# The last layer's first feed-forward product in seven block products instead of eight

## The chip, the cores and the metric

The kernel runs on one core of one Trainium2 chip. The metric is the device time of one execution in microseconds (us). The engines go by these names in the rows: PE is TensorE (matmuls), PEld its weight loads, DVE is VectorE, ACT is ScalarE, POOL is GpSimd, SP is SyncE, which issues the DMA transfers.

## The reference

The program is one inference step through a trunk of two layers over 640 tokens (512 latent tokens and 128 context tokens), 1024 channels wide. Each layer has four token mixers and then a gated feed-forward part. The change touches only the feed-forward part of the second, last layer:

```python
h2 = rms_norm(x) * (1 + sc2) + sh2
a, gate_ffn = jnp.split(h2 @ p['w_ffn_in'], 2, axis=-1)
x = x + g2 * ((jax.nn.silu(gate_ffn) * a) @ p['w_ffn_out'])
```

`w_ffn_in` has 1024 rows (k) and 2 x 2816 columns, a linear and a gate half; `w_ffn_out` has 2816 rows and 1024 columns. After the last layer `y = rms_norm(x, final_gain)`. Everything is float32.

## The kernel before

**Numbers in two parts.** Every fp32 operand of a large product is split in a high part (rounded to the type that the rows call fp32r, on ACT, L84) and a low part (the difference, on VectorE, L176, for weights L123). A product is three matmuls per 128 rows of k: high by high, high by low, low by high. Tokens lie along the columns, channels along the 128 partitions.

**Feed-forward part.** The function `layer` works it off as follows. `out` is the output projection with its residual; `norm_mod` (L1047 to L1061) computes the modulated norm of one half of the tokens into the tiles `hh` and `hl` and runs woven with `out` and with the first two hidden blocks. The halves are 384 and 256 columns (`HALVES`). `hidden(j)` makes one of 22 blocks of 128 hidden columns: it loads the gate block `wg` and the linear block `wa` (`wload`: a 512 KB DMA into a raw buffer `wraw`, of which there are two; the high part `whi` by ACT and the low part `wlo` by VectorE, three buffers each). Then for each half: 24 matmuls with the gate (k has 8 tiles), tanh on ACT (L1210), one VectorE step (L1211), 24 matmuls with the linear block, one VectorE step (L1213), and the split of the result into `fh` and `fl`. So a block has 96 matmuls, 48 of 384 columns and 48 of 256.

**Groups.** Hidden blocks come in groups of 8, 8 and 6 (`KGROUPS`). After each of the first two groups `back` multiplies the group by `w_f2` (eight row blocks, each loaded by `wload`, 128 x 1024) and adds the result to the residual `x` (`resid`, L1070). The last group's `w_f2` blocks are kept in `wkh` and `wkl`, and its products run woven with the final norm.

**What sets the order.** A scheduler places each engine's instructions by its own estimates, near the order in which the program is written; `weave` mixes two streams in the program itself. Each engine then runs its list strictly in order and waits on semaphores. Buffers of a pool come free when their last reader is done; a DMA into a buffer waits on SP for that.

**PSUM.** Matmul results go to three tiles of 512 columns named `psg`, three named `pst` and one of 1024 named `pss`.

The functions that the diff touches:

Of the kernel before, what the change touches and what calls it, by code (L numbers as in the profile page):

```python
# [64 lines left out]
class Trunk:  # L65
# [1113 lines left out]
    def layer(self, l, hs, first):  # L1179
# [20 lines left out]
        def hidden(j, halves, tiles):  # L1200
            if tiles is None:
                tiles = fs[j] = self.u("fh", F32R), self.u("fl", F32R)
            hi, lo = tiles
            wg = self.wload(A["w_f1"][l, j, 1], 8, 128)
            wa = self.wload(A["w_f1"][l, j, 0], 8, 128)
            for c0, c1 in halves:
                y, tg = self.u("fy"), self.u("ft")
                n = c1 - c0
                pg = self.gemm(wg, hs, c0, c1)
                nc.scalar.activation(tg[:, 0:n], pg, AF.Tanh, scale=0.5)  # L1210
                nc.vector.scalar_tensor_tensor(tg[:, 0:n], tg[:, 0:n], 1.0, pg, op0=ALU.add, op1=ALU.mult)  # L1211
                pa = self.gemm(wa, hs, c0, c1)
                nc.vector.scalar_tensor_tensor(y[:, 0:n], tg[:, 0:n], 0.5, pa, op0=ALU.mult, op1=ALU.mult)  # L1213
                self.split(hi[:, c0:c1], lo[:, c0:c1], y[:, 0:n])
                self.drop(y, tg)
                yield 48 * n

        def some(half):
            for j in range(2):
                yield from hidden(j, (half,), fs.get(j))  # L1220

        fs = {}
        n0, n1 = (c1 - c0 for c0, c1 in HALVES)
        sum(out(*HALVES[0]))
        self.weave(self.norm_mod(hs, x, l, 24, 32, *HALVES[0]), out(*HALVES[1]), 8 * 24 * n1, 6)
        self.drop(ms)
        self.weave(self.norm_mod(hs, x, l, 24, 32, *HALVES[1]), some(HALVES[0]), 96 * n0, 6)
        sum(some(HALVES[1]))
        nxt = l + 1 < self.depth
        def ada():  # L1230
            if l == 0:
                yield from self.ada_tail(0, 40, 48, 2, 4, True)
            if nxt:
# [2 lines left out]
        ada = ada()

        def back(halves, last=False):
            for m in range(8):
                if last:  # L1240
                    if len(ws) <= m:
                        self.wload(A["w_f2"][l, m, :, g0:g1], g1 - g0, 128, kept=ws)
                    w = [z.rearrange("p (a b) -> p a b", b=128) for z in ws[m]]
                else:
                    w = self.wload(A["w_f2"][l, m, :, g0:g1], g1 - g0, 128)
                for c0, c1 in halves:
                    self.resid(x[m], self.gemm(w, [fs[j] for j in range(g0, g1)], c0, c1), l, 40, m, c0, c1)
                    yield 3 * (g1 - g0) * (c1 - c0)
# [287 lines left out]
```

## Time and profile before

| | us |
|---|---|
| Median of three runs (lowest, highest) | 3148.22 (3145.90, 3150.94) |
| The profiled execution | 3147.23 |
| Its span, first to last instruction | 3145.3 |
| TensorE busy in the span | 3038.9 (97%) |
| VectorE busy | 2174.5 (69%) |
| ACT busy | 1464.8 (47%) |
| GpSimd busy | 285.7 (9%) |

The mean granted clock of TensorE is 0.996 of full speed. The shares are means over stages that differ, attention and scan on the one side and large products on the other. Durations in the rows come from the one profiled execution.

### The profile page before, as it was taken

To read this page: it belongs to the slowest core of one execution; us is meant where nothing else is said; L and a number is where in the kernel's file an instruction comes from. 1 tells how busy PE (TensorE), PEld (TensorE's weight loads), DVE (VectorE), ACT (ScalarE), POOL (GpSimd) and SP (SyncE) were. 2 spreads that over 40 slices of the span, in tenths; PEclk is the share of its full clock that TensorE was granted. 3 is DMA by queue.
4 is the path that set the end of the run, shared out by engine and by line. 5 is a ranking of instruction groups with operands and counts; after the bars stand their busy time and mean duration, and the time that the engine had idled before them with its cause. 6 is when DMAs were issued, how large, how long until landed. Compare 5 with 4: busy or idle time off the path is not lost.

```text
span 3145.3 us, 54163 instructions
## 1 busy us (share of the span) xinstructions
PE 3038.9 (97%) x20898; PEld 2928.7 (93%) x20898; DVE 2174.5 (69%) x4894; ACT 1464.8 (47%) x3088; POOL 285.7 (9%) x301
## 2 busy tenths in 40 slices
...
GB/s 217 91 88 112 99 101 65 79 96 86 46 39 61 134 154 165 150 154 154 159 85 61 59 71 74 70 56 100 98 62 38 51 69 158 97 81 74 75 78 70
DMA packets 135121, 297.16 MB, mean 94 GB/s; under 512 B 15888, under 2 KB 53584, under 8 KB 134864
## 3 DMA queue, kind: packets, MB, share of 16 engines
...
## 4 chain that ended last, share of the span: by engine, by line
PE 71%; DVE 15%; ACT 5%; issue 4%; DMA 3%; POOL 1%; SPq 0%; DVEq 0%; ACTq 0%; POOLq 0%
PE psg L78 58%; PE pss L78 7%; PE pst L81 2%; PE pst L78 2%; DVE wlo L123 2%; ACT P L235 2%; DVE pl L176 1%; DMA ada<-in_w_ada 1%; DVE trash L984 1%; DVE sm L218 1%; DVE P L232 1%; DMA wraw<-in_w_f 1%; ACT whi L84 1%; PE pst L167 1%; DVE nx L1054 1%
## 5 line engine op out<-in xcount | busy, mean ns | idle before, releaser
L78 PE MATMUL psg<-hh,whi 128*128 128x384 f32 (+1 forms) x3776 | 1119.4, 315 | 9.8 <-DVE ft L1211 4.7
L78 PE MATMUL psg<-hl,whi 128*128 128x384 f32 (+1 forms) x3776 | 1108.2, 312 | 2.9 <-DVE hl L1056 2.3
L78 PEld LDWEIGHTS psg<-hh,whi 128*128 128x128 f32 x3776 | 715.8, 190 | 13.2 <-DVE ft L1211 5.3
L78 PEld LDWEIGHTS psg<-hl,whi 128*128 128x128 f32 x3776 | 716.3, 190 | 5.3 <-DVE hl L1056 3.0
L78 PE MATMUL psg<-hh,wlo 128*128 128x384 f32 (+1 forms) x3744 | 648.9, 312 | 0.0
L84 ACT ACTIVATE whi<-wraw 128x1024 fp32r<-128x1024 f32 (+3 forms) x402 | 380.9, 948 | 462.0 <-PE psg L78 366.7
L78 PEld LDWEIGHTS psg<-hh,wlo 128*128 128x128 f32 x3744 | 569.6, 190 | 0.1
L123 DVE TENSOR_TENSOR wlo<-wraw,whi 128x1024 fp32r<-128x1024 f32 (+3 forms) x398 | 453.5, 1140 | 125.3 <-ACT whi L84 111.1
L235 ACT ACTIVATE P<-pss,sm 128x768 f32<-128x768 f32 (+2 forms) x240 | 162.9, 680 | 208.7 <-DVE sm L218 120.9
L176 DVE TENSOR_TENSOR pl<-pst,ph 128x384 fp32r<-128x384 f32 (+2 forms) x408 | 196.8, 510 | 21.4 <-ACT ph L84 17.5
L84 ACT ACTIVATE ph<-pst 128x384 fp32r<-128x384 f32 (+2 forms) x408 | 170.7, 457 | 52.5 <-PE pst L81 49.1
L81 PE MATMUL pst<-ident,P 128*128 128x128 f32 x1104 | 168.8, 276 | 20.5 <-DVE of L242 15.4
L1070 DVE SCALAR_TENSOR_TENSOR xr<-psg,mod,xr 128x128 f32<-128x128 f32 (+1 forms) x192 | 78.5, 435 | 151.1 <-PE psg L78 151.1
L81 PEld LDWEIGHTS pst<-ident,P 128*128 128x128 f32 x1104 | 125.5, 141 | 36.2 <-DVE of L242 21.2
L984 DVE CUSTOM_DVE_ANT_0 yada<-ada 128x512 f32<-128x512 f32 x224 | 154.4, 689 | 5.1
L78 PE MATMUL psg<-oTh,whi 128*128 128x384 f32 (+1 forms) x512 | 152.1, 315 | 0.1
L218 DVE TENSOR_REDUCE sm<-pss 128x1 f32<-128x768 f32 x128 | 121.9, 952 | 42.9 <-PE pss L78 41.8
L78 PE MATMUL psg<-oTl,whi 128*128 128x384 f32 (+1 forms) x512 | 151.5, 312 | 0.0
L78 PE MATMUL psg<-fh,whi 128*128 128x256 f32 (+1 forms) x512 | 148.2, 309 | 0.0
L78 PE MATMUL psg<-fl,whi 128*128 128x256 f32 (+1 forms) x512 | 148.2, 309 | 0.0
L84 ACT ACTIVATE fh<-fy 128x384 fp32r<-128x384 f32 (+1 forms) x88 | 41.5, 471 | 179.1 <-DVE fy L1213 179.1
L1213 DVE SCALAR_TENSOR_TENSOR fy<-ft,psg 128x384 f32<-128x384 f32 (+1 forms) x88 | 42.9, 487 | 111.9 <-PE psg L78 111.3
...
## 6 DMA issues: line engine op xcount, KB each, us to landing
wraw<-in_w_f SPq DMA_DIRECT2D x128, 512.0 KB, 3.4
...
ada<-in_w_ada SPq DMA_DIRECT2D x112, 256.0 KB, 3.0
wraw<-in_w_br SPq DMA_DIRECT2D x64, 256.0 KB, 2.6
...
```

The lines of the kernel that those rows point to most:

```text
L78: self.nc.tensor.matmul(out, lhsT, rhs, start=start, stop=stop)
L81: self.nc.tensor.transpose(out, in_, self.ident)
L84: self.nc.scalar.activation(out, in_, AF.Copy, scale=scale)
L123: nc.vector.tensor_sub(lo[:, :n], raw[:, :n], self.r(hi[:, :n]))
L167: self.nc.tensor.transpose(ps[:, i * rows : (i + 1) * rows], t[:rows, c0 + i * 128 : c0 + (i + 1) * 128], self.ident[:rows, :rows])
L176: self.nc.vector.tensor_sub(lo, src, self.r(hi))
L218: nc.vector.tensor_reduce(nm, S[:, 0:n], axis=AX.X, op=ALU.max, negate=True)
L232: nc.vector.tensor_scalar_mul(P[:, p0 : p0 + n], P[:, p0 : p0 + n], l)
L235: self.nc.scalar.activation(P, S, AF.Exp, bias=nm, accum_out=l)
L984: nc.vector.tensor_tensor_reduce(out=y, in0=w, in1=c, scale=1.0, scalar=0.0, op0=ALU.mult, op1=ALU.add, accum_out=acc[:, b, k, j : j + 1])
L1070: self.nc.vector.scalar_tensor_tensor(x[:, a:b], ps[:, a - c0 : b - c0], mod[:, b_g + m, j : j + 1], x[:, a:b], op0=ALU.mult, op1=ALU.add)
L1213: nc.vector.scalar_tensor_tensor(y[:, 0:n], tg[:, 0:n], 0.5, pa, op0=ALU.mult, op1=ALU.mult)
```

## The change

In the last layer the tokens are cut into two equal halves of 320 (`EVEN`). Blocks 0 and 1 are computed as before, but in these halves. For each block j from 2 to 21 the weight is seen as two by two blocks: gate and linear by the lower and upper half of k (four k tiles each). a11 is the gate with k tiles 0 to 3, a12 the gate with 4 to 7, a21 and a22 the same of the linear weight. The tokens give b11, b12 (lower k, first and second half of tokens) and b21, b22 (upper k). Seven products of 12 matmuls of 320 columns replace eight: 84 matmuls a block. For that, GpSimd makes four combinations of the weights (s1 = a21 + a22, s2 = s1 - a11, s3 = a11 - a21, s4 = a12 - s2) per block, and these and the plain blocks are split; four combinations of the tokens (t1 = b12 - b11, t2 = b22 - t1, t3 = b22 - b12, t4 = b21 - t2) are made and split once (`sums`), woven with the second half of blocks 0 and 1. The results are put together by copies from PSUM on ACT (c11, c12, c22) and adds on VectorE. `norm_even` keeps the norm in fp32 beside its split. The groups are four, of 5, 6, 6 and 5 blocks (`SGROUPS`), so there are three `back` passes before the kept one, not two. The first layer's code is only moved into functions (`back`, `glu`, `hidden`, `ffn`). Lines up to the feed-forward part stand two or three further down (L78 is now L80, L84 L86, L123 L125, L176 L178, L1070 L1073).

The core of the diff:

```diff
+EVEN = ((0, 320), (320, 640))
...
+SGROUPS = ((0, 5), (5, 11), (11, 17), (17, 22))
...
-        nt = n // 128
+        at = [min(i, n - 128) for i in range(0, n, 128)]
+        nt = len(at)
...
-        for g0, g1 in KGROUPS:
-            for j in range(max(g0, 2), g1):
-                sum(hidden(j, HALVES, None))
-                for _ in range(4):
-                    next(ada, None)
-            if g1 < NH:
-                sum(back(HALVES))
-                self.drop([fs[j] for j in range(g0, g1)])
...
+            ada, groups = ada(), KGROUPS
+            last = self.ffn(l, x, ms, out, fs, ada)
+        else:
+            ada, groups = iter(()), SGROUPS
+            last = self.ffn7(l, x, ms, out, fs)
+        g0, g1 = groups[-1]
...
+    def glu(self, hi, lo, y, g, a):
+        nc = self.nc
+        nc.scalar.activation(y, g, AF.Tanh, scale=0.5)
+        nc.vector.scalar_tensor_tensor(y, y, 1.0, g, op0=ALU.add, op1=ALU.mult)
+        nc.vector.scalar_tensor_tensor(y, y, 0.5, a() if callable(a) else a, op0=ALU.mult, op1=ALU.mult)
+        self.split(hi, lo, y)
...
+    def norm_even(self, B, H, x, l, half):
...
+            hi, lo = B[k][:, 0:320], B[k][:, 320:640]
+            if even:
+                self.cp(hi, h)
+            else:
+                nc.vector.tensor_copy(hi, h)
+            nc.vector.tensor_sub(lo, h, self.r(hi))
...
+    def ffn7(self, l, x, ms, out, fs):
+        nc, A = self.nc, self.A
+        H = [self.u("hf") for _ in range(8)]
+        B0 = [self.u("b0", F32R) for _ in range(8)]
+        B1 = [None] * 8
+        hx = lambda c0, c1: [(t[:, 0:320], t[:, 320:640]) for t in (B1 if c0 else B0)]
+        def some(half):
+            for j in range(2):
+                yield from self.hidden(l, j, hx, (EVEN[half],), fs)
+        sum(out(*EVEN[0]))
+        self.weave(self.norm_even(B0, H, x, l, 0), out(*EVEN[1]), 8 * 24 * 320, 6)
+        self.drop(ms)
+        B1[:] = [self.u("b1", F32R) for _ in range(8)]
+        self.weave(self.norm_even(B1, H, x, l, 1), some(0), 96 * 320, 6)
+        T = [[self.u("bt", F32R) for _ in range(4)] for _ in range(4)]
+        def sums():
+            for k in range(4):
+                b11, b12 = H[k][:, 0:320], H[k][:, 320:640]
+                b21, b22 = H[k + 4][:, 0:320], H[k + 4][:, 320:640]
+                t = self.u("tt"), self.u("tt")
+                t1, t2, t3, t4 = t[0][:, 0:320], t[0][:, 320:640], t[1][:, 0:320], t[1][:, 320:640]
+                nc.vector.tensor_sub(t1, b12, b11)
+                nc.gpsimd.tensor_sub(t3, b22, b12)
+                nc.vector.tensor_sub(t2, b22, t1)
+                nc.gpsimd.tensor_sub(t4, b21, t2)
+                for i, z in enumerate((t1, t2, t3, t4)):
+                    self.split(T[i][k][:, 0:320], T[i][k][:, 320:640], z)
+                    if i % 2:
+                        yield 1
+                self.drop(t)
+        self.weave(sums(), some(1), 96 * 320, 8)
+        self.drop(H, B1[0:4])
+        right = {"b11": B0[0:4], "b21": B0[4:8], "b22": B1[4:8], "t1": T[0], "t2": T[1], "t3": T[2], "t4": T[3]}
+        def mul(ps, w, b, first):
+            hi, lo = w
+            todo = [(z, i, k) for z, ids in ((hi, (0, 1)), (lo, (0,))) for k in range(4) for i in ids]
+            for n, (z, i, k) in enumerate(todo):
+                nc.tensor.matmul(ps, z[:, k * 128 : (k + 1) * 128], right[b][k][:, i * 320 : i * 320 + 320],
+                                 start=first and n == 0, stop=n == 11, skip_group_check=True)
+        W = {}
+        def load(j):
+            w = W[j] = {}
+            for i, n in ((1, "g"), (0, "a")):
+                w[n] = self.sb.tile([128, 1024], F32, name="wraw", tag="wraw", bufs=2)
+                nc.sync.dma_start(w[n].rearrange("p (a b) -> p a b", a=8), A["w_f1"][l, j, i])
+            s1, s2 = w["s"] = [self.u("ws", F32, 512) for _ in range(2)]
+            g, a = w["g"], w["a"]
+            nc.gpsimd.tensor_add(s1, a[:, 0:512], a[:, 512:1024])
+            nc.gpsimd.tensor_sub(s2, s1, g[:, 0:512])
+        def load2(j):
+            w = W[j]
+            s3, s4 = s = [self.u("ws", F32, 512) for _ in range(2)]
+            g, a = w["g"], w["a"]
+            nc.gpsimd.tensor_sub(s3, g[:, 0:512], a[:, 0:512])
+            nc.gpsimd.tensor_sub(s4, g[:, 512:1024], w["s"][1])
+            w["s"] += s
+        def two(j, x, y, srcs):
+            hi = self.sb.tile([128, 1024], F32R, name="whi", tag="whi", bufs=3)
+            lo = self.sb.tile([128, 1024], F32R, name="wlo", tag="wlo", bufs=3)
+            for i, z in enumerate(srcs):
+                n = z.shape[-1]
+                self.split(hi[:, i * n : i * n + n], lo[:, i * n : i * n + n], z)
+            W[j][x], W[j][y] = ((hi[:, i : i + 512], lo[:, i : i + 512]) for i in (0, 512))
+        def first(j):
+            two(j, "a11", "a12", [W[j]["g"]])
+        def second(j):
+            t = W[j]["t"] = self.u("wh", F32R, 512), self.u("wl", F32R, 512)
+            self.split(t[0], t[1], W[j]["a"][:, 512:1024])
+        def third(j):
+            two(j, "s2", "s1", [W[j]["s"][1], W[j]["s"][0]])
+            self.drop(W[j]["s"][0:2])
+        def fourth(j):
+            two(j, "s3", "s4", [W[j]["s"][2], W[j]["s"][3]])
+            self.drop(W[j]["s"][2:4])
+        V = {}
+        def head(j):
+            v = V[j] = {"q": self.psg()[:, 0:320], "t": (self.u("fu"), self.u("fv"))}
+            v["c11"], v["c12"], v["c22"] = v["t"][0][:, 0:320], v["t"][0][:, 320:640], v["t"][1][:, 0:320]
+            fs[j] = self.u("fh", F32R), self.u("fl", F32R)
+            mul(v["q"], W[j]["a11"], "b11", True)
+            self.cp(v["c11"], v["q"])
+        def head2(j):
+            v = V[j]
+            p = self.pst()[:, 0:320]
+            mul(p, W[j]["a12"], "b21", True)
+            nc.vector.tensor_add(v["c11"], v["c11"], p)
+            y = v["t"][1][:, 320:640]
+            nc.scalar.activation(y, v["c11"], AF.Tanh, scale=0.5)
+            nc.vector.scalar_tensor_tensor(y, y, 1.0, v["c11"], op0=ALU.add, op1=ALU.mult)
+        def tail(j):
+            v = V[j]
+            mul(v["q"], W[j]["t"], "t4", False)
+            self.drop(W[j]["t"])
+            y = v["t"][1][:, 320:640]
+            nc.vector.scalar_tensor_tensor(y, y, 0.5, v["q"], op0=ALU.mult, op1=ALU.mult)
+            self.split(fs[j][0][:, 0:320], fs[j][1][:, 0:320], y)
+        def tail2(j):
+            v = V.pop(j)
+            mul(v["r"], W[j]["s4"], "b22", False)
+            del W[j]
+            nc.vector.tensor_add(v["c12"], v["c12"], v["r"])
+            self.glu(fs[j][0][:, 320:640], fs[j][1][:, 320:640], v["t"][0][:, 0:320], v["c12"], v["c22"])
+            self.drop(v["t"])
+        load(2)
+        load2(2)
+        first(2)
+        second(2)
+        group = 0
+        for j in range(2, NH + 1):
+            if j < NH:
+                third(j)
+                head(j)
+                if j + 1 < NH:
+                    load(j + 1)
+            if j - 1 in V:
+                tail(j - 1)
+            if j < NH:
+                head2(j)
+            if j - 1 in V:
+                tail2(j - 1)
+            g0, g1 = SGROUPS[group]
+            if j == g1 and j < NH:
+                sum(self.back(l, x, fs, g0, g1, HALVES))
+                self.drop([fs[i] for i in range(g0, g1)])
+                group += 1
+            if j == NH:
+                break
+            v = V[j]
+            fourth(j)
+            if j + 1 < NH:
+                load2(j + 1)
+            mul(v["q"], W[j]["s2"], "t2", False)
+            self.cp(v["c12"], v["q"])
+            if j + 1 < NH:
+                first(j + 1)
+            v["r"] = self.pst()[:, 0:320]
+            mul(v["r"], W[j]["s1"], "t1", True)
+            if j + 1 < NH:
+                second(j + 1)
+            mul(v["q"], W[j]["s3"], "t3", False)
+            self.cp(v["c22"], v["q"])
+            nc.vector.tensor_add(v["c22"], v["c22"], v["r"])
+        self.drop(B0, B1[4:8], T)
```

In the order of the changed kernel `head` is the product A11·B11 and its copy c11, `head2` A12·B21, `tail` A22·T4, `tail2` S4·B22.

VectorE, one block in the middle of the loop, before (`ft` and `fy` are the gated value, `fl` its low part, `wlo` the low parts of the gate and linear weights):

```order
L1211 SCALAR_TENSOR_TENSOR ft<-ft,psg 128x384
L1213 SCALAR_TENSOR_TENSOR fy<-ft,psg 128x384
L176 TENSOR_TENSOR fl<-fy,fh 128x384
L123 TENSOR_TENSOR wlo<-wraw,whi 128x1024
L1211 SCALAR_TENSOR_TENSOR ft<-ft,psg 128x256
L1213 SCALAR_TENSOR_TENSOR fy<-ft,psg 128x256
L123 TENSOR_TENSOR wlo<-wraw,whi 128x1024
L176 TENSOR_TENSOR fl<-fy,fh 128x256
```

The same place in the changed kernel, twelve rows of a block, which the rows of c22's add (L1500) and of the glu's first half (L1451) complete (`fu` and `fv` hold c11, c12, c22 and the value; `ws` are GpSimd's combinations, `wraw` the raw weights):

```order
L178 TENSOR_TENSOR fl<-fv,fh 128x320
L1441 TENSOR_TENSOR fu<-fu,pst 128x320
L178 TENSOR_TENSOR wlo<-ws,whi 128x512
L1444 SCALAR_TENSOR_TENSOR fv<-fv,fu 128x320
L178 TENSOR_TENSOR wlo<-ws,whi 128x512
L1458 TENSOR_TENSOR fu<-fu,pst 128x320
L178 TENSOR_TENSOR wlo<-wraw,whi 128x1024
L1256 SCALAR_TENSOR_TENSOR fu<-fu 128x320
L1257 SCALAR_TENSOR_TENSOR fu<-fu,fv 128x320
L178 TENSOR_TENSOR fl<-fu,fh 128x320
L178 TENSOR_TENSOR wlo<-ws,whi 128x512 x2
L178 TENSOR_TENSOR wl<-wraw,wh 128x512
```

Eight instructions became fourteen, most of them shorter; five of them are splits of 512 columns, which stand between the steps that lead from one PSUM bank to the next.

ACT at the end of the first group, before (`wraw_31286` and higher are the blocks of `w_f2`, each loaded into one of the two raw buffers; `ft` and `fh` belong to blocks 6 and 7 of the hidden columns):

```order
L84 ACTIVATE whi_31287<-wraw_31286 128x1024
L84 ACTIVATE fh_31030<-fy_31101 128x256
L1210 ACTIVATE ft_31173<-psg_31174 128x384
L84 ACTIVATE fh_31158<-fy_31172 128x384
L84 ACTIVATE whi_31346<-wraw_31345 128x1024
L1210 ACTIVATE ft_31230<-psg_31231 128x256
L84 ACTIVATE whi_31405<-wraw_31404 128x1024
L84 ACTIVATE fh_31158<-fy_31229 128x256
L84 ACTIVATE whi_31464<-wraw_31463 128x1024
```

ACT at the end of the first group in the changed kernel (`wraw_30970` and `wraw_30972` are the gate and linear weights of block 6, `wraw_31027` to `wraw_31314` the eight blocks of `w_f2`, `ws` combinations of block 5's weights):

```order
L86 ACTIVATE wh_31395<-wraw_30972 128x512
L86 ACTIVATE whi_31028<-wraw_31027 128x640
L86 ACTIVATE whi_31069<-wraw_31068 128x640
L86 ACTIVATE whi_31110<-wraw_31109 128x640
L86 ACTIVATE whi_31151<-wraw_31150 128x640
L86 ACTIVATE whi_31192<-wraw_31191 128x640
L86 ACTIVATE whi_31233<-wraw_31232 128x640
L86 ACTIVATE whi_31274<-wraw_31273 128x640
L86 ACTIVATE whi_31315<-wraw_31314 128x640
L86 ACTIVATE whi_31355<-ws_30894 128x512
L86 ACTIVATE whi_31355<-ws_30895 128x512
L86 ACTIVATE whi_31378<-wraw_30970 128x1024
```

The splits of `w_f2` moved from between the last block's steps to one row behind the other, behind the split of half of block 6's linear weight and ahead of the split of its gate weight. On SP the eight loads of `w_f2` stand right behind the two loads of block 6's weights.

## Rows read from the trace of the kernel before

**Rows 1.** The page's chain of waits, shares of the span by engine.
```profile
PE 71%; DVE 15%; ACT 5%; issue 4%; DMA 3%; POOL 1%; SPq 0%; DVEq 0%; ACTq 0%; POOLq 0%
```

**Rows 2.** Windows: length, busy PE, PEld, DVE, ACT, POOL, clock, DMA, GB/s.
```profile
2660.00:2700.00 40.00, 37.36 (x249) 36.05 (x248) 34.05 (x68) 28.51 (x50) 4.24 (x5) 1.00 0.45 148
2700.00:3090.00 390.00, 390.00 (x2666) 390.00 (x2665) 143.20 (x226) 95.96 (x139) 0.00 (x0) 1.00 0.25 79
```

**Rows 3.** Timeline of VectorE, one block: start, length, instruction [idle before, releaser].
```profile
2701.45 0.55 DVE L1211 SCALAR_TENSOR_TENSOR ft<-ft,psg 128x384 f32<-128x384 f32 x1 [0.48 <-ACT ft L1210]
2705.09 0.56 DVE L1213 SCALAR_TENSOR_TENSOR fy<-ft,psg 128x384 f32<-128x384 f32 x1 [3.08 <-PE psg L78]
2706.23 0.56 DVE L176 TENSOR_TENSOR fl<-fy,fh 128x384 fp32r<-128x384 f32 x1 [0.59 <-ACT fh L84]
...
2711.17 1.22 DVE L123 TENSOR_TENSOR wlo<-wraw,whi 128x1024 fp32r<-128x1024 f32 x1
2712.31 0.42 DVE L176 TENSOR_TENSOR fl<-fy,fh 128x256 fp32r<-128x256 f32 x1
2715.52 0.56 DVE L1211 SCALAR_TENSOR_TENSOR ft<-ft,psg 128x384 f32<-128x384 f32 x1 [2.79 <-ACT ft L1210]
```

**Rows 4.** Timeline of TensorE, starts of the products of the same block.
```profile
2700.73 0.33 PE L78 MATMUL psg<-hh,whi 128*128 128x384 f32 x1
...
2704.89 0.28 PE L78 MATMUL psg<-hh,whi 128*128 128x256 f32 x1
...
2707.76 0.28 PE L78 MATMUL psg<-hh,whi 128*128 128x256 f32 x1
```

**Rows 5.** Groups by shape, 2500 to 3146 us: count, busy us, mean ns, idle before.
```profile
L176 DVE TENSOR_TENSOR fl<-fy,fh 128x384 fp32r<-128x384 f32 x22 | 12.3, 558 | 12.0 <-ACT fh L84 12.0
...
L84 ACT ACTIVATE fh<-fy 128x384 fp32r<-128x384 f32 x22 | 11.5, 525 | 82.4 <-DVE fy L1213 82.4
...
L176 DVE TENSOR_TENSOR fl<-fy,fh 128x256 fp32r<-128x256 f32 x22 | 9.2, 420 | 1.5 <-ACT fh L84 1.5
...
L123 DVE TENSOR_TENSOR wlo<-wraw,whi 128x512 fp32r<-128x512 f32 x9 | 6.2, 688 | 5.4 <-ACT whi L84 5.3
...
L84 ACT ACTIVATE whi<-wraw 128x512 fp32r<-128x512 f32 x9 | 5.7, 633 | 7.3 <-PE psg L78 5.0 <-issue 1.4 <-ACT ph L84 0.8
```

**Rows 6.** GpSimd's lines L817 and L915: ns minimum/median/maximum, first and last start.
```profile
L817 POOL TENSOR_TENSOR hk<-hk,hT x56: 726/795/1371, 332.4 to 2106.1; 128x320 f32<-128x320 f32 x56
...
L915 POOL TENSOR_TENSOR gt<-gt x32: 1553/1571/2079, 600.7 to 2523.0; 128x640 f32<-128x640 f32 x32
```

**Rows 7.** Timeline of GpSimd, 2652 to 2682 us.
```profile
2653.64 1.01 POOL L1047 TENSOR_TENSOR nx<-xr,nacc 128x384 f32<-128x384 f32 x1 [2.42 <-DVE hl L1056]
...
2676.61 3.75 POOL L1047 TENSOR_TENSOR nx<-xr,nacc 128x256 f32<-128x256 f32 x4 [16.12 <-ACT nacc L84]
```

**Rows 8.** Timeline of VectorE beside them.
```profile
2652.95 0.61 DVE L1056 SCALAR_TENSOR_TENSOR hl<-nx,mod,hh 128x384 fp32r<-128x384 f32 x1
...
2654.00 1.07 DVE L1056 SCALAR_TENSOR_TENSOR hl<-nx,mod,hh 128x384 fp32r<-128x384 f32 x1
...
2677.44 3.33 DVE L1054 SCALAR_TENSOR_TENSOR nx<-xr,mod,nacc 128x128 f32<-128x128 f32 x5
```

**Rows 9.** VectorE's line L176 over the whole span: ns minimum/median/maximum.
```profile
L176 DVE TENSOR_TENSOR pl<-pst,ph x408: 270/547/559, 140.8 to 2560.3; 128x384 fp32r<-128x384 f32 x100, 128x256 fp32r<-128x256 f32 x30, 128x128 fp32r<-128x128 f32 x6
...
L176 DVE TENSOR_TENSOR oTl<-of,oTh x32: 787/820/2183, 319.2 to 2564.7; 128x640 fp32r<-128x640 f32 x32
```

**Rows 10.** DMA issues: count, KB each, median us to landing.
```profile
wraw<-in_w_br SPq DMA_DIRECT2D x64, 256.0 KB, 2.6
...
wraw<-in_w_f SPq DMA_DIRECT2D x16, 384.0 KB, 3.2
```

**Rows 11.** Windows at the kernel's start, columns as in rows 2.
```profile
40.00:45.00 5.00, 1.53 (x7) 0.51 (x5) 4.97 (x5) 4.29 (x8) 3.95 (x4) 1.00 0.00 0
45.00:49.00 4.00, 3.39 (x11) 3.39 (x12) 4.00 (x11) 2.01 (x4) 0.00 (x0) 0.57 0.40 132
```

More of the change, by code (lines that the diff above doesn't have):

```diff
@@ L1198, in out @@
                 yield 24 * (c1 - c0)
[L1200 to L1233, printed above, removed]
-                yield from self.ada_tail(l + 1, 0, 48, 2, 4, True)
@@ L1236, in layer @@
[L1236 to L1248, printed above, removed]
-                if g1 < NH:
-                    for _ in range(2):
-                        next(ada, None)
@@ new lines, in glu, with hidden @@
+    def glu(self, hi, lo, y, g, a):
[4 more added lines that the diff above has]
+        self.split(hi, lo, y)
+    def hidden(self, l, j, hx, halves, fs):
+        if j not in fs:
+            fs[j] = self.u("fh", F32R), self.u("fl", F32R)
+        hi, lo = fs[j]
+        wg = self.wload(self.A["w_f1"][l, j, 1], 8, 128)
+        wa = self.wload(self.A["w_f1"][l, j, 0], 8, 128)
+        for c0, c1 in halves:
+            n = c1 - c0
+            y = self.u("fy")
+            h = hx(c0, c1)
+            pg = self.gemm(wg, h, 0, n)
+            self.glu(hi[:, c0:c1], lo[:, c0:c1], y[:, 0:n], pg, lambda: self.gemm(wa, h, 0, n))
+            self.drop(y)
+            yield 48 * n
```

84 lines of the change are left out of this document (73 added, 11 removed).

## The prediction

> **What bounds the kernel now.** I read the chain of waits first, then the window table of the part that changes, then the timelines of TensorE, VectorE and GpSimd there. The chain [rows 1] runs 71% on TensorE; VectorE follows with 15%. The window table [rows 2] shows where the last layer's feed-forward stands: in 2700 to 3090 us TensorE is busy 390.00 of 390 us while VectorE is busy 143.20 and GpSimd not at all. In 2660 to 2700, where the second half of the norm runs beside the first blocks, TensorE idles 2.6 of 40 us and VectorE is already busy 34.05. So in the loop only TensorE's own work counts, and VectorE and ACT have much room. One block lasts from 2701.45 to 2715.52, 14.07 us [rows 3].
>
> **What is removed.** A block before is 48 matmuls of 384 columns and 48 of 256. 24 of 384 start from 2700.73 to 2704.89, 0.1733 us apart, 24 of 256 from 2704.89 to 2707.76, 0.1196 apart [rows 4]. No row shows 320 columns; the bounds are these two, and since 0.1733 to 0.1196 goes almost as 384 to 256, I take their mean, 0.1465. Seven products of 12 are 84 x 0.1465 = 12.3 us (bounds 10.0 and 14.6). Twenty blocks: 20 x (14.07 - 12.3) = -35.3 us, if TensorE never waits.
>
> **What is added in each block.** VectorE gets five splits of 512 columns at 0.69 [rows 5], one of 1024 at 1.22 [rows 3] and nine instructions of 320 at 0.49, the mean of 0.558 and 0.420 [rows 5]: 9.06 us, against some 5.4 before (two each of 0.56, 0.42 and 1.22 and the two fl of rows 5). Consecutive ones overlap by 0.08 (the 1.22 from 2711.17 end at 2712.39, and the next one starts at 2712.31 [rows 3]), so VectorE alone needs 7.9 of 12.3. ACT passes of 320 cost 0.46 (0.525 for 384, less in VectorE's ratio of 0.49 to 0.558), of 512 0.63 [rows 5]; seven, five and one of 1024 are some 7.3 us, so ACT still has room. GpSimd gets four adds of 512 columns. No such row exists; 320 columns take 0.73 at least and 640 1.55 [rows 6], so 1.25 each, 5.0 a block (bounds 2.9 and 6.2).
>
> These would fit side by side, but the trace shows that they do not run side by side. While GpSimd worked from 2653.64 and 2676.61 [rows 7], VectorE's hl went from 0.61 to 1.07 us, and five instructions of 128 columns took 3.33 beside GpSimd's 3.75 [rows 8]. The two alternate. Those that read PSUM are spared: pl, read from PSUM, x408, never exceeds 559 ns, while oTl, with both inputs in SBUF, has a median of 820 and a maximum of 2183 [rows 9]. Of the new VectorE work, only four instructions of 320 (1.96 us) read PSUM, so 9.06 - 1.96 + 5.0 = 12.1 us a block exclude each other, just under 12.3.
>
> The Trainium skill's page "SBUF — State Buffer", section "Who interferes with whom", says the same more strictly: a VectorE instruction with two SBUF inputs and a GpSimd instruction lock each other out, one with a single SBUF input does not. This trace agrees (559 against 2183 ns). By the rule alone, with nothing else waiting, the block would stay bound by TensorE, which is rival A below.
>
> I laid one block's VectorE and GpSimd rows against TensorE's order by hand. The order leaves no slack: the copy of c12 on ACT, which TensorE needs before S3·T3 can use its bank, stands behind a tanh that waits for the add of c12 on VectorE, and this stands behind two splits that GpSimd holds up; likewise the copy of c22 before A22·T4. A block behind a group border finds GpSimd's work done and takes 12.3. The next take 13.9, 13.6, then 14.2: 7.9 of VectorE, 3.9 of GpSimd's 5.0 exposed, 2.4 of waits for ACT and TensorE. Bounds: 12.3 (hidden) and 15.3 (all 5.0 exposed). Over 2, 5, 5 and 4 transitions without a border the excess is 1.7 + 6.8 + 6.8 + 3.7 = **+19.0 us** (bounds 0 and 48).
>
> **The three group borders.** Before, ACT splits the w_f2 blocks two ahead among the last hidden block's work, and TensorE has no gap. After, both raw weight buffers hold block j+1's gate and linear weights when the border comes; the gate's is read by a split which ACT's order places behind all eight w_f2 splits. So the first w_f2 load waits on SP until the linear buffer is free, and that is read last by the low half `wl`, at the end of the chain behind S4·B22: add 0.49, tanh 0.46, two glu steps 0.98, split 0.46, ACT split 0.63, low half 0.69 [rows 5], seven hand-overs of 0.06 (fy ends 2705.65, an ACT pass of 0.525, fl starts 2706.23 [rows 3, 5]): 4.1. Then 0.9 for one GpSimd step in between, the load of 320 KB 2.9 (256 KB 2.6, 384 KB 3.2 [rows 10]) and the ACT split of 640 columns 0.74 (0.633 for 512 and 0.108 more per 128 [rows 5]). TensorE has two products of 1.76 left, 3.5, and then idles 4.1 + 0.9 + 2.9 + 0.74 - 3.5 = 5.2 (rounded); A22·T4 behind the border waits another 0.7 for a copy behind two ACT splits (between 0 and 1.3). 3 x 5.9 = **+17.7** (bounds 0, if the load is early, and 3 x 8 if POOL holds up two more steps). The eight loads then pass through a single buffer: 2.9 + 0.74 + 0.82 (the median of oTl [rows 9]) = 4.5 against TensorE's 15 x (0.1733 + 0.1196) = 4.4 in the first group: **+1.3** at most.
>
> After a gap TensorE may run slower. In 40 to 45 us it was busy 1.53 of 5 us, and from 45 to 49 the granted clock was 0.57 [rows 11], part of it the 1.2 GHz level: 4 x 0.43 = 1.7 us lost. At three borders: **+5.1** (bounds 0 and 5.1).
>
> **Before the loop and behind it.** 2660 to 2700 gains 16 splits and eight sums on VectorE, 24 x 0.49 = 11.8, less 0.08 of overlap each, 9.8; the first block's low halves 1.22 + 3 x 0.69 = 3.3; GpSimd gains eight steps of 0.73 and four of 1.25, 11, half of it exposed. VectorE had 6 us free there [rows 2], and products of T2 wait for the last of it: 9.8 + 3.3 + 5.5 - 6 = 12.6, of which blocks 0 and 1 cover some; I take **+9** (bounds 3 and 13). The last block's tail is longer by an add: **+0.5**.
>
> **Sum.** -35.3 + 19.0 + 17.7 + 1.3 + 5.1 + 9 + 0.5 = +17.3 on the profiled execution of 3147.23, 3164.5. The median of the runs is 3148.22, 1.0 more: 3165.
>
> **Rivals.**
> *A, faster.* The alternation costs little because GpSimd's steps fall beside PSUM-reading work and VectorE's idle time. For it: 12.1 under 12.3, and VectorE's 7.9 alone leave 4.4. Against: the order ties ACT's copies to VectorE's blocked splits. Without the excess, with borders without the 0.9 of GpSimd (15.0) and 4 before the loop: -35.3 + 15.0 + 1.3 + 5.1 + 4 + 0.5 = -9.4, 3139.
> *B, about the same.* Half of the excess (9.5) and the borders at 15.0, no fall of the clock because two products still run into each gap, 4 before the loop: -35.3 + 9.5 + 15.0 + 1.3 + 4 + 0.5 = -5.0, 3143. Against: the gap of rows 11 has some work in it too.
> *C, much slower.* GpSimd's steps hold VectorE up for 4.8 us a block rather than 3.9, so that the 16 transitions take 14.4 on the mean and not 13.5: excess 34, before the loop 13: -35.3 + 34 + 17.7 + 1.3 + 5.1 + 13 + 0.5 = +36, 3184. For it: `nx x5` beside GpSimd was blocked almost all along. It decides from the point where GpSimd's add takes 1.5 rather than 1.25 us.
> *D, the work saved is not there.* If 320 columns were spaced like 384, a block has 14.6 us, and the change loses about 45: nothing speaks for it, since 256 to 384 goes with the columns.
>
> **How the numbers follow.** Forecast 0.55, A 0.20, B 0.18, C 0.06, D 0.01. About 0.2% (6.3 us) can be told from no change: faster is below 3141.9, slower above 3154.5. A is faster but for a tenth, B the same but for a sixth, the forecast (3155 to 3178 by itself) slower but for a few: faster 0.21, same 0.20, slower 0.59. The range reaches from A's time to C's, 3138 to 3184.
>
> **What would show it.** In the changed kernel's loop: matmuls of 320 spaced 0.147 where TensorE does not wait (the 12.3); GpSimd's adds of 512 at 1.25 and VectorE's splits `wlo<-ws` well above 0.69 beside them; idle time of TensorE before S3·T3 and A22·T4, released by ACT's copies; blocks of 13.6 to 14.2. At three places a gap of TensorE of some 5 us, ended by a w_f2 load and its split, and a granted clock under 1 behind it. I am wrong if the blocks take 12.3 to 12.6 throughout (A), or if w_f2's first load lands before S1·T1 ends.

## The result: slower by 1.2%

| | median of runs (us) | lowest to highest | profiled span |
|---|---|---|---|
| before | 3149.58 | 3145.90 to 3152.75 | 3145.3 |
| changed kernel | 3187.12 | 3182.29 to 3189.68 | 3180.5 |

The ratio is 1.0118 (95% interval 1.0100 to 1.0135). The profiled execution of the changed kernel took 3182.29 us, its span is 35.2 us longer than before's (it is the shortest of its four; the medians are 37.5 apart). 3165 was forecast, in a range up to 3184.

### The profile page after: what moved, and what is told of

The parts are those of the page before. It is cut to its first block, busy times and chain, and to the rows that moved or that the text cites. A ratio compares the mean times of both kernels' runs of the same rounds, so it can differ in the third digit from the quotient of the medians.

```text
span 3180.5 us, 54251 instructions
## 1 busy us (share of the span) xinstructions
PE 3025.5 (95%) x20662; PEld 2907.5 (91%) x20662; DVE 2312.4 (73%) x5087; ACT 1535.4 (48%) x3260; POOL 418.8 (13%) x389
## 4 chain that ended last, share of the span: by engine, by line
PE 67%; DVE 18%; ACT 7%; DMA 4%; issue 4%; POOL 1%; SPq 0%; DVEq 0%; ACTq 0%; POOLq 0%
PE psg L80 49%; PE pss L80 7%; PE psg L1380 3%; PE pst L83 2%; PE pst L80 2%; DVE wlo L125 2%; PE pst L1380 2%; ACT P L237 2%; DVE pl L178 1%; DMA wraw<-in_w_f 1%; ACT whi L86 1%; DVE wlo L178 1%; DVE P L234 1%; DVE sm L220 1%; DVE trash L986 1%
## 5 line engine op out<-in xcount | busy, mean ns | idle before, releaser
L80 PE MATMUL psg<-hh,whi 128*128 128x256 f32 (+1 forms) x3072 | 913.3, 315 | 5.9 <-DVE fy L1256 1.7
L80 PE MATMUL psg<-hl,whi 128*128 128x256 f32 (+1 forms) x3072 | 902.0, 312 | 2.8 <-DVE hl L1059 2.3
L80 PEld LDWEIGHTS psg<-hh,whi 128*128 128x128 f32 x3072 | 580.8, 189 | 8.4 <-ACT gt L894 2.2
L80 PEld LDWEIGHTS psg<-hl,whi 128*128 128x128 f32 x3072 | 581.3, 189 | 4.7 <-DVE hl L1059 2.8
L86 ACT ACTIVATE whi<-wraw 128x1024 fp32r<-128x1024 f32 (+5 forms) x390 | 362.0, 929 | 431.1 <-PE psg L80 253.0
L80 PE MATMUL psg<-hh,wlo 128*128 128x384 f32 (+1 forms) x3040 | 532.3, 313 | 0.0
L125 DVE TENSOR_TENSOR wlo<-wraw,whi 128x1024 fp32r<-128x1024 f32 (+5 forms) x366 | 407.1, 1113 | 145.1 <-ACT whi L86 130.7
L80 PEld LDWEIGHTS psg<-hh,wlo 128*128 128x128 f32 x3040 | 463.4, 190 | 0.0
L178 DVE TENSOR_TENSOR pl<-pst,ph 128x384 fp32r<-128x384 f32 (+2 forms) x408 | 196.9, 510 | 21.4 <-ACT ph L86 17.8
L86 ACT ACTIVATE ph<-pst 128x384 fp32r<-128x384 f32 (+2 forms) x408 | 170.7, 457 | 52.1 <-PE pst L83 48.8
L80 PE MATMUL psg<-fh,whi 128*128 128x256 f32 (+1 forms) x528 | 157.4, 317 | 20.6 <-ACT whi L86 20.1
L1073 DVE SCALAR_TENSOR_TENSOR xr<-psg,mod,xr 128x128 f32<-128x128 f32 (+3 forms) x216 | 88.2, 435 | 102.5 <-PE psg L80 102.2
L80 PE MATMUL psg<-fl,whi 128*128 128x256 f32 (+1 forms) x528 | 156.7, 315 | 0.0
L80 PE MATMUL psg<-oTh,whi 128*128 128x384 f32 (+1 forms) x512 | 152.0, 314 | 0.1
L80 PE MATMUL psg<-oTl,whi 128*128 128x384 f32 (+1 forms) x512 | 151.4, 312 | 0.0
L80 PEld LDWEIGHTS psg<-fh,whi 128*128 128x128 f32 x528 | 102.1, 193 | 21.8 <-ACT whi L86 20.9
L234 DVE TENSOR_SCALAR P<-P,sm 128x768 f32<-128x768 f32 (+1 forms) x192 | 113.4, 591 | 4.1
```

Of the source, the lines that this page charges most:

```text
L80: self.nc.tensor.matmul(out, lhsT, rhs, start=start, stop=stop)
L86: self.nc.scalar.activation(out, in_, AF.Copy, scale=scale)
L125: nc.vector.tensor_sub(lo[:, :n], raw[:, :n], self.r(hi[:, :n]))
L178: self.nc.vector.tensor_sub(lo, src, self.r(hi))
L234: nc.vector.tensor_scalar_mul(P[:, p0 : p0 + n], P[:, p0 : p0 + n], l)
L1073: self.nc.vector.scalar_tensor_tensor(x[:, a:b], ps[:, a - c0 : b - c0], mod[:, b_g + m, j : j + 1], x[:, a:b], op0=ALU.mult, op1=ALU.add)
```

## The profile after

The chain of waits runs a little less on TensorE than in [rows 1], and more on the engines that feed it:

```profile
PE 67%; DVE 18%; ACT 7%; DMA 4%; issue 4%; POOL 1%; SPq 0%; DVEq 0%; ACTq 0%; POOLq 0%
```

The windows of [rows 2], columns as there. TensorE now idles 10 of 40 us ahead of the loop and 39 of 390 in it, and its granted clock is below 1 in both:

```profile
2660.00:2700.00 40.00, 29.83 (x179) 28.26 (x178) 34.18 (x67) 29.52 (x59) 15.74 (x11) 0.92 0.24 79
2700.00:3090.00 390.00, 350.70 (x2268) 344.58 (x2268) 245.59 (x362) 138.38 (x251) 110.95 (x75) 0.96 0.24 75
```

**The saving is there.** TensorE's timeline behind the first border, the starts of S3·T3, from one of which to the next is one block of 84 matmuls. Without a wait a block takes 12.29 us, 0.1463 per matmul. The third block, where TensorE waits, takes 14.08:

```profile
2809.36 0.89 PE L1380 MATMUL psg<-bt,whi 128*128 128x320 f32 x5
...
2821.65 1.33 PE L1380 MATMUL psg<-bt,whi 128*128 128x320 f32 x8
...
2833.94 1.33 PE L1380 MATMUL psg<-bt,whi 128*128 128x320 f32 x8
...
2848.02 1.46 PE L1380 MATMUL psg<-bt,whi 128*128 128x320 f32 x8 [1.63 <-ACT fu L86]
```

**Why that block is late.** VectorE and GpSimd in the same block. GpSimd's four steps run from 2840.16 to 2846.19. Beside them VectorE's steps with two inputs in SBUF last 1.4 to 1.8 us (0.49 to 0.69 just ahead of them and behind); those that read PSUM (L1441, L1458) stay at 0.48. (A block has fifteen VectorE instructions, as the prediction's 9.06 us counts them, and not fourteen.)

```profile
2840.43 1.40 DVE L178 TENSOR_TENSOR fl<-fv,fh 128x320 fp32r<-128x320 f32 x1 [0.54 <-ACT fh L86]
2841.75 0.48 DVE L1441 TENSOR_TENSOR fu<-fu,pst 128x320 f32<-128x320 f32 x1
2842.15 1.39 DVE L178 TENSOR_TENSOR wlo<-ws,whi 128x512 fp32r<-128x512 f32 x1
2843.46 1.58 DVE L1444 SCALAR_TENSOR_TENSOR fv<-fv,fu 128x320 f32<-128x320 f32 x1
2844.97 1.77 DVE L178 TENSOR_TENSOR wlo<-ws,whi 128x512 fp32r<-128x512 f32 x1
2846.66 0.48 DVE L1458 TENSOR_TENSOR fu<-fu,pst 128x320 f32<-128x320 f32 x1
```
```profile
2840.16 1.32 POOL L1393 TENSOR_TENSOR ws<-wraw 128x512 f32<-128x512 f32 x1 [10.37 <-DMA wraw<-in_w_f]
2841.43 1.55 POOL L1400 TENSOR_TENSOR ws<-wraw 128x512 f32<-128x512 f32 x1
2842.95 1.74 POOL L1394 TENSOR_TENSOR ws<-ws,wraw 128x512 f32<-128x512 f32 x1
2844.77 1.42 POOL L1401 TENSOR_TENSOR ws<-wraw,ws 128x512 f32<-128x512 f32 x1
```

Over the whole loop the means are these:

```profile
L1444 DVE SCALAR_TENSOR_TENSOR fv<-fv,fu 128x320 f32<-128x320 f32 x20 | 20.6, 1028 | 1.6 <-ACT fv L1443 1.6
...
L1441 DVE TENSOR_TENSOR fu<-fu,pst 128x320 f32<-128x320 f32 x20 | 9.7, 484 | 4.1 <-PE pst L1380 4.0
```

ACT waits for the add of the previous block's c12, and the copy of this block's c12 (`fu<-psg`) stands behind the tanh; when it has been made TensorE goes on at 2848.02:

```profile
2847.18 0.47 ACT L1255 ACTIVATE fu<-fu 128x320 f32<-128x320 f32 x1 [3.49 <-DVE fu L1458]
2847.55 0.42 ACT L86 ACTIVATE fu<-psg 128x320 f32<-128x320 f32 x1
```

**Where GpSimd's work falls.** The two blocks ahead of the late one have the same four steps, and take 12.29. GpSimd starts them 1.8 and 2.7 us behind S3·T3, in the late block 6.2 behind it, when the weights have landed:

```profile
2811.12 1.41 POOL L1393 TENSOR_TENSOR ws<-wraw 128x512 f32<-128x512 f32 x1 [47.21 <-DMA wraw<-in_w_f]
...
2824.31 1.29 POOL L1393 TENSOR_TENSOR ws<-wraw 128x512 f32<-128x512 f32 x1 [7.90 <-DVE wlo L178]
```

**A border.** The low half `wl` frees a raw buffer at 2766.67, SP issues the first w_f2 load at 2766.74, ACT splits it at 2769.62 behind 3.67 us of waiting, and TensorE has idled 6.75 us. Behind the gap the granted clock is 0.51 for 5.3 us, nearly all of it the 1.2 GHz level:

```profile
2765.98 0.69 DVE L178 TENSOR_TENSOR wl<-wraw,wh 128x512 fp32r<-128x512 f32 x1 [0.70 <-ACT wh L86]
```
```profile
2769.62 0.74 ACT L86 ACTIVATE whi<-wraw 128x640 fp32r<-128x640 f32 x1 [3.67 <-DMA wraw<-in_w_f]
```
```profile
2770.41 0.69 PE L80 MATMUL psg<-fh,whi 128*128 128x384 f32 x1 [6.75 <-ACT whi L86]
```
```profile
2770.40:2775.70 5.30, 5.29 (x17) 5.29 (x18) 1.52 (x2) 0.74 (x1) 0.00 (x0) 0.51 0.21 62
```

**The way into the loop.** Here the forecast had a hole. GpSimd starts the combinations of block 2 while VectorE still splits token sums and weights, and these stretch from 0.49 and 0.69 to 1.5 and 1.75 us. TensorE waits 2.64 and 2.99 us, and the clock falls again:

```profile
2709.17 3.04 DVE L178 TENSOR_TENSOR bt<-tt,bt 128x320 fp32r<-128x320 f32 x2
2712.14 1.75 DVE L178 TENSOR_TENSOR wl<-wraw,wh 128x512 fp32r<-128x512 f32 x1
```
```profile
2712.91 1.48 PE L1380 MATMUL psg<-bt,whi 128*128 128x320 f32 x8 [2.64 <-ACT fu L86]
...
2725.00 2.50 PE L1380 MATMUL psg<-bt,wh 128*128 128x320 f32 x8 [2.99 <-ACT fv L86]
```
```profile
2725.00:2731.00 6.00, 6.00 (x22) 6.00 (x23) 2.27 (x4) 1.00 (x3) 2.78 (x3) 0.50 0.24 89
```

What these two waits end on is not a split of VectorE. It is ACT, which stands waiting for GpSimd's results; the copies of c11 and c22 come behind the split of a combination:

```profile
2711.90 0.63 ACT L86 ACTIVATE whi<-ws 128x512 fp32r<-128x512 f32 x1 [2.33 <-POOL ws L1394]
2712.43 0.42 ACT L86 ACTIVATE fu<-psg 128x320 f32<-128x320 f32 x1
...
2724.00 0.63 ACT L86 ACTIVATE whi<-ws 128x512 fp32r<-128x512 f32 x1 [2.73 <-POOL ws L1394]
2724.53 0.42 ACT L86 ACTIVATE fv<-psg 128x320 f32<-128x320 f32 x1
```

In the late block above ACT's splits of `ws` wait for no combination; there it is VectorE that is held.

**Where the 35 us come from**, from the starts of products (twelve matmuls of 320 are 1.756 us; "too long" is the time less the products in it):

| term | forecast | measured |
|---|---|---|
| 20 blocks at 12.29 rather than 14.07 | -35.3 | -35.6 |
| block 2 starts at 2706.24, before at 2700.73 - 24 x 0.1733 = 2696.57 [rows 4] | +9 | +9.7 |
| way into the loop: 2706.24 to 2736.69, eleven products | 1.7 (first group) | +11.1 |
| later blocks between the borders, too long by 2.39 (rest of the first group), 6.77, 7.26, 2.10 | 17.3 | +18.5 |
| idle at borders, 6.75 + 6.56 + 6.79 | +17.7 | +20.1 |
| w_f2 passes: 39.0, 45.1, 44.9 against 35.2, 42.2, 42.2 | +6.4 | +9.4 |
| kept pass and tail | +0.5 | +2.0 |
| sum | +17.3 | +35.2 |

## The experiments

Each was timed beside the kernel before, and the ratio is to that. The medians of the kernel before on these occasions lie between 3144.6 and 3149.6, so differences between two rows, or to the changed kernel's 3187, are good to some 5 us only.

| run | median us | ratio (95%) |
|---|---|---|
| e1 combinations left out | 3137.19 | 0.9965 (0.9954 to 0.9976) |
| e2 combinations on VectorE | 3156.38 | 1.0034 (1.0021 to 1.0047) |
| e3 loads behind the border | 3159.00 | 1.0044 (1.0027 to 1.0060) |
| e4 filler products | 3185.49 | 1.0124 (1.0109 to 1.0139) |
| e5 = e2 and e3 | 3126.34 | 0.9940 (0.9927 to 0.9954) |
| e6 = e5, token sums on VectorE | 3125.26 | 0.9935 (0.9922 to 0.9947) |
| e7 = e6, norm on VectorE | 3122.11 | 0.9925 (0.9911 to 0.9938) |
| e8 blocks 2 and 3 on VectorE | 3174.58 | 1.0089 (1.0071 to 1.0107) |
| e9 results unread | 3146.88 | 1.0006 (0.9996 to 1.0015) |
| e10 linear split early | 3190.14 | 1.0137 (1.0120 to 1.0154) |
| e11 GpSimd early | 3144.89 | 0.9992 (0.9982 to 1.0001) |
| e12 GpSimd late | 3181.75 | 1.0102 (1.0087 to 1.0117) |

**e1 and e2: GpSimd's combinations.**

```diff
-            nc.gpsimd.tensor_add(s1, a[:, 0:512], a[:, 512:1024])
-            nc.gpsimd.tensor_sub(s2, s1, g[:, 0:512])
...
+            w["s"] = fixed
...
-            nc.gpsimd.tensor_add(s1, a[:, 0:512], a[:, 512:1024])
...
+            nc.vector.tensor_add(s1, a[:, 0:512], a[:, 512:1024])
```
(The first edit is e1, in which the splits read four tiles that are filled once. The second is e2, which does the same with s2, s3 and s4.)

> GpSimd's four combinations per block are left out: the splits of third and fourth read four fixed tiles that are filled once, so the output is not the reference's; VectorE and ACT do the same work as in the changed kernel. Theory (GpSimd and VectorE exclude each other): no block over 12.5 us, VectorE's tanh chain at a border 2 us shorter, the entry into the loop shorter; 18 + 6 + some 5 us less than the changed kernel's 3187, so 3155 to 3163. Rival (VectorE's fourteen instructions in this order are too long by themselves): blocks of 13.6 to 14.2 stay, 3180 or more.

> The four combinations per block move from GpSimd to VectorE, four more instructions of 0.69 us. Theory: VectorE needs some 10.4 us of 12.3 and nothing is shared, so most of the 18 us in the blocks goes: 3162 to 3172. Rival (VectorE's own length in this order): blocks longer than before, 3187 to 3200.

e1 came out at 3137, 50 us under the changed kernel, e2 at 3156, 31 under it; both more than expected. VectorE's 80 splits of 512 columns, in the changed kernel, in e1 and in e2:

```profile
L178 DVE TENSOR_TENSOR wlo<-ws,whi 128x512 fp32r<-128x512 f32 x80 | 71.9, 921 | 2.4 <-ACT whi L86 1.8
```
```profile
L178 DVE TENSOR_TENSOR wlo<-ws,whi 128x512 fp32r<-128x512 f32 x80 | 52.8, 686 | 0.9 <-ACT whi L86 0.4
```
```profile
L178 DVE TENSOR_TENSOR wlo<-ws,whi 128x512 fp32r<-128x512 f32 x80 | 53.0, 684 | 0.2
```

In e2 VectorE does more (busy 262 of the 390 us from 2700, 246 in the changed kernel), but each of its splits is shorter: blocks take 12.3 to 12.6 us, and the way into the loop falls from 30.5 to 20.3 us. The rival (VectorE too long by itself) is out. The border gaps stay in e2, at 5.3, 5.9 and 6.6 us, so GpSimd's blocking is only a part of them (in e1 they go: nothing but the plain splits reads the raw buffers, and ACT's order has the linear split ahead of the tanh):

```profile
2758.63 0.69 PE L80 MATMUL psg<-fh,whi 128*128 128x384 f32 x1 [5.27 <-ACT whi L86]
```

**e3: the border.**

```diff
-                if j + 1 < NH:
+                if j + 1 < NH and j != SGROUPS[group][1]:
                     load(j + 1)
...
                 group += 1
+                load(j + 1)
```

> At the three group borders the next block's two weight loads (and its GpSimd combinations) come behind the w_f2 pass, not ahead of it; all else as in the changed kernel. Theory (w_f2's first load waits for a raw buffer that the next block's weights hold): the three gaps of 6.6 to 6.8 us go, and with them the 5.3 us at half clock behind each and the single-buffer pace: 20 + 8 + 1.5 less, 3155 to 3162. Rival (the gap is the chain from S4·B22 to the residual or GpSimd's work): gaps of over 3 us stay, 3175 or more; or the next block's first product waits for its late weights by some 5 us at each border, 3170.

3159, as expected: no gap of TensorE at any border, and no wait for the next block's late weights. The raw buffer is the cause.

**e4: the clock behind the gap.**

```diff
             if j == g1 and j < NH:
+                p = self.pst()[:, 0:320]
+                for _ in range(3):
+                    mul(p, (B0[0], B0[1]), "b11", True)
```

> Three products of 12 matmuls (5.3 us) on tiles that are there anyway are added on TensorE at each border, into a bank that nobody reads; the w_f2 load is as late as before. Theory (the first 5.3 us behind the gap run at 1.2 GHz because TensorE idled): the gap shrinks to some 1.5 us, the clock stays up, and 2.6 us a border come back: 3178 to 3181. Rival (the w_f2 pass is slow because its loads go through one buffer): the pass keeps its 39 and 45 us, 3187.

Neither: 1.6 us less than the changed kernel, within the spread of the runs. The clock stayed at full behind the first and the third border and the passes took 38.2, 44.6 and 42.8 us, 3.4 less together; in the first pass TensorE now ran into the loads, which come through one buffer 4.7 us apart. Clock and pace hide each other, and the experiment doesn't price the clock by itself.

**e5, e6, e7: the causes together.**

```diff
-                nc.gpsimd.tensor_sub(t3, b22, b12)
+                nc.vector.tensor_sub(t3, b22, b12)
...
-                nc.gpsimd.tensor_mul(h, x[k][:, c0:c1], R[:, 0:320])
+                nc.vector.tensor_mul(h, x[k][:, c0:c1], R[:, 0:320])
```
(The first edit, with t4 too, is e6; the second is added in e7.)

> The edits of e2 (combinations on VectorE) and e3 (next block's loads behind the w_f2 pass at a border) together. Theory (two separate causes): e2's 3156 less its three border gaps of 5.3 to 6.6 us and some 5 us of half clock behind them: 3130 to 3136, faster than before. Rival (the gaps return in another place, as waits of TensorE for the next block's combinations, which VectorE now has to make behind the w_f2 pass): 3140 to 3150.

> e5 with the two token sums t3 and t4 made by VectorE too, so that GpSimd does nothing behind the norm. Theory (in the changed kernel GpSimd's first sum took 5.9 us beside VectorE, and ACT's splits, and behind them block 1's weights, waited for it: the 4.85 us gap of TensorE): the gap goes, with its half clock behind it, 5 to 7 us less than e5. Rival (VectorE is full there, 34 of 40 us, and the sums only move the wait): within 2 us of e5.

> e6 with the multiplications of the norm (odd k) on VectorE, so that the last feed-forward part has no work on GpSimd at all. Theory: VectorE's seven norm steps, 4.8 us beside GpSimd in the changed kernel, take 2.5, but four multiplications of 0.49 in each half are added: 0 to 3 us less than e6. Rival: VectorE is the longer chain in the norm and it gets slower by 1 to 4 us.

e5: 3126, faster than before and under its range; e2 and e3 add up (31 + 28 = 59, and 61 measured). e6 is 1.1 less than e5, which is within the spread: the rival was right, the gap of 4.86 us went but waits of 1.85 (for VectorE's low half) and 2.12 took its place. e7 is 3.1 less than e6, as its theory says, but the intervals of the two overlap, so that step is not shown. By its median e7 is the fastest version, 0.75% under the kernel before. Its loop is bound by TensorE again:

```profile
2700.00:3070.00 370.00, 368.94 (x2499) 366.20 (x2499) 262.42 (x480) 158.64 (x286) 0.00 (x0) 1.00 0.25 83
```

**e8: the way into the loop.**

```diff
-            nc.gpsimd.tensor_add(s1, a[:, 0:512], a[:, 512:1024])
...
+            (nc.vector if j < 4 else nc.gpsimd).tensor_add(s1, a[:, 0:512], a[:, 512:1024])
```
(And so for s2, s3 and s4.)

> The combinations of blocks 2 and 3 alone move from GpSimd to VectorE; blocks 4 to 21 as in the changed kernel. Theory (the entry into the loop, 30.5 us for eleven products of 19.3, is GpSimd's first eight combinations beside VectorE's last token splits, and half clock behind each gap; the prediction had no term for it): 8 to 10 us less than the changed kernel's 3187, 3176 to 3180. Rival (VectorE has simply too much to do there, with its token splits): under 3 us, 3184 or more.

12.5 us less than the changed kernel by the medians, 9 when each is taken against the kernel before beside it, and 5.0 between the two profiled executions. In the profile the eleven products of the way in take 20.5 us rather than 30.5, so the term that the prediction lacked is GpSimd's work in the first two blocks. But part of it only moves on: the next block, now the first with GpSimd's combinations, takes 18.4 us, where it took 13.6. VectorE has no token splits left there; ACT waits for a combination as before:

```profile
2730.74 1.15 ACT L86 ACTIVATE whi<-ws 128x512 fp32r<-128x512 f32 x2 [3.48 <-POOL ws L1394]
```

So VectorE's token splits are not needed for this cost.

**e9, e11, e12: amount or place.** Fixed tiles as in e1, and GpSimd's work comes back with results that nobody reads: in e9 at its old trigger, in e11 and e12 (from block 4 on) started by another add.

```diff
+            nc.gpsimd.tensor_add(z[:, 0:128], c[:, 0:128], fixed[0][:, 0:128])
+            for i in range(4):
+                nc.gpsimd.tensor_add(z, fixed[i % 2], fixed[1 - i % 2])
```
(c is c22 in e11 and c11 in e12.)

> As e1 (splits read two fixed tiles, output not the reference's), but GpSimd makes its four combinations of each block into tiles that nobody reads: against e1 only GpSimd's work comes back, not the waits for its results. Theory (the engines exclude each other): blocks of 13.6 to 14.2 and the slow entry come back, 18 to 30 us over e1's 3137: 3155 to 3170. Rival (in the changed kernel the splits waited for GpSimd's results): within 5 us of e1.

> As e1 (fixed tiles in place of the combinations, output not the reference's), and from block 4 on GpSimd makes one add of 128 and four of 512 columns per block into a tile that nobody reads, started by the add of c22, that is at the end of S3·T3. VectorE's order is the same in e11 and e12. Theory (the place decides): GpSimd is done by about the add of c12's tanh chain, blocks stay at 12.3 to 12.7, 0 to 8 us over e1's 3137: 3137 to 3145. Rival (the amount decides): e11 and e12 within 5 us of each other.

> As e11, but GpSimd's five adds per block are started by the add of c11, at the end of A12·B21, where the chain from c11 to c12 runs; amount and VectorE's order as in e11. Theory (the place decides): blocks of 13.5 to 14.2 come back, 18 blocks by 1 to 1.9 us: 18 to 34 us over e1, 3155 to 3171. Rival (the amount decides): within 5 us of e11.

e9 fell between theory and rival, 10 us over e1. In the profiles most of it lies ahead of block 4's S3·T3: the first eighteen products of the loop take 45.1 us, in the changed kernel 44.1 and in e1 33.3. So the way in is slow even when nobody reads the results. What held VectorE, awaited results and late loads have in it each is not separated. The later blocks took 12.3 to 12.5 us, but for one of 13.1, although VectorE was stretched (`wlo<-ws` 831 ns on the mean, `fl<-fv` 1311): GpSimd started 3.3 us behind S3·T3, in the late block shown above 6.2 behind it.

```profile
2806.24 1.33 PE L1380 MATMUL psg<-bt,whi 128*128 128x320 f32 x8
```
```profile
2809.52 1.30 POOL L1398 TENSOR_TENSOR ws<-wraw 128x512 f32<-128x512 f32 x1 [44.69 <-DMA wraw<-in_w_f]
```

So I ran e11 and e12, with the same amount of work at two places: 3145 and 3182. The place decides. In e11 blocks took 12.3 to 13.4, mostly 13.2, which is more than expected; in e12 mostly 14.4 to 16.0, more than expected too. In e12 the glu steps behind c12 are held, and TensorE waits for the copy of c22 behind them:

```profile
L1256 DVE SCALAR_TENSOR_TENSOR fu<-fu 128x320 f32<-128x320 f32 x18 | 27.2, 1514 | 1.2 <-ACT fu L1255 1.2
```
```profile
2842.82 1.43 PE L1380 MATMUL psg<-bt,wh 128*128 128x320 f32 x8 [1.87 <-ACT fv L86]
```

**e10: the same by another order.**

```diff
-            t = W[j]["t"] = self.u("wh", F32R, 512), self.u("wl", F32R, 512)
+            t = W[j]["t"] = pairs[j % 2]
...
             if j + 1 < NH:
+                second(j + 1)
                 first(j + 1)
```

> The changed kernel with the split of the upper half of the linear weight placed ahead of the split of the gate weight (its two tiles are kept for good, so that it need not wait for old ones); GpSimd's and VectorE's work is the same. In the changed kernel this split's low half ended 4 us behind the gate's and held the raw buffer, so that GpSimd's four steps started 4 us later, beside the chain of tanh steps. Refined theory (it is not the amount of exclusion that costs, but that GpSimd's steps fall on the chain from c11 to c12): GpSimd starts 3 to 4 us earlier in a block, and at least two thirds of the 18 us in the blocks go, and some of each border gap: 3160 to 3173. Rival (the amount decides: VectorE is stretched by 42 us in all wherever GpSimd works): 3180 or more.

It failed, and not as the rival says: GpSimd did not start earlier, since its step s3 now came last and kept the raw buffer. The weights land later, ACT waits for them ahead of a tanh, and the gaps at the borders grow to 10.4 to 11.8 us:

```profile
2844.00 0.63 ACT L86 ACTIVATE wh<-wraw 128x512 fp32r<-128x512 f32 x1 [3.78 <-DMA wraw<-in_w_f]
```
```profile
2772.60 0.69 PE L80 MATMUL psg<-fh,whi 128*128 128x384 f32 x1 [11.78 <-ACT whi L86]
```

## Why the prediction was wrong

- **The side was right, the size not.** +17.3 was forecast and +35.2 measured on the profiled execution. The step that failed is the excess over the blocks: "Over 2, 5, 5 and 4 transitions without a border the excess is 1.7 + 6.8 + 6.8 + 3.7". For the first group it took GpSimd's and VectorE's work of a block in the middle, where a block "behind a group border finds GpSimd's work done". At the start of the loop it was not done: GpSimd made the combinations of block 2 while the loop was already running, held VectorE, and ACT stood waiting for its results ahead of the copies that TensorE needed. That cost 11.1 + 2.4 rather than 1.7, 11.8 of the missing 17.9 us. e8 moved only that work and took 10.0 us off the way in, of which the next block gave 4.8 back.
- **Block of 12.3**: right (12.29).
- **Excess in the later groups**: 16.1 against 17.3, by the chain that was named, but the closeness is partly luck. The prediction priced the amount of GpSimd's work; e11 and e12 show that its place decides. Behind a border GpSimd's work is not "done", as the prediction had it; it falls early in the block (2811.12 above). So two blocks in a row stay at 12.3, one more at 12.8, and the others take 12.5 to 15.7. GpSimd's price of 1.25 holds where nothing is beside it (1.29 to 1.32); over all blocks, with VectorE beside it, the four means are 1.45 to 1.57.
- **Rival A's reasoning** (12.1 just under 12.3) is possible in principle, as e9's blocks show, but not where this order puts GpSimd. The Trainium skill's page "SBUF — State Buffer", section "Who interferes with whom", says that a VectorE instruction with two inputs in SBUF contends with GpSimd, and that one with at most one such input, as those that read PSUM here, does not. This trace agrees: L1441 had a mean of 484 ns, L1444 with two inputs in SBUF 1028 (490 in e2).
- **Borders**: mechanism right (e3), size low by 5.4. The gaps are 6.6 to 6.8 and not 5.2. At the first border GpSimd held both glu steps of the chain (1.56 and 1.46 us, 2 us and not 0.9), which is most of the difference there; e2, with these steps on VectorE, still has gaps of 5.3 to 6.6, so GpSimd is not all of it; the rest is open. The wait of 0.7 ahead of A22·T4 did not come. The 5.3 us at 0.51 cost 2.6 and not 1.7 us each. The +1.3 for the single buffer does not follow from the prediction's own figures (4.46 against 4.39 us a load, some 0.5 over eight loads); beyond the clock the passes lost some 1.6.
- **Ahead of the loop**: 9.7 against 9, by luck. Ahead of all that the change touches, at 2561 us, the profiled execution of the changed kernel was already 2.2 us ahead of before's (the traces of all runs scatter by 5 us there), so the stage itself is 11.9 longer, nearer to the 12.6 that the prediction worked out than to the 9 that it took; and it is so by another wait than T2's. GpSimd's first token sum took 5.87 us, ACT's token splits waited for it, and block 1's weights stood behind them on ACT (TensorE idle 4.85).
- **The tail**: 2.0 against 0.5. TensorE's wait for the sums of the final norm is 1.0 longer (2.62 for 1.61); the rest was not looked into.
- The range ended at 3184 because rival C let GpSimd's work be exposed inside the loop and ahead of it, not on the way in.
